# A decoder trunk in split float32: the first pass of each MLP takes two blocks by seven products, with a turned K tile and a split matmul in every fast pass

## The chip, the cores and the metric

The kernel runs on one core of one Trainium2 chip. The core has TensorE (matmuls, with a unit of its own for loading weights, PEld in the profile), VectorE (DVE), ScalarE (ACT), GpSimd (POOL), SyncE (SP), which issues the loads, and 16 DMA engines. Matmuls write into eight banks of PSUM, each 128 partitions by 512 float32 values. The metric is the time of one execution on the device, in microseconds (us).

## The reference

The input is 256 tokens of 2048 values. One layer mixes by a gated short convolution, one by multi-head latent attention; each is followed by an MLP with 8192 hidden values, and after each mixer and each MLP stands a layer norm of `ALPHA * x + f(x)`. The change touches the two MLPs alone:

```python
def sq_relu_mlp(x, w1, w2):
    return jnp.square(jax.nn.relu(x @ w1)) @ w2

for layer in range(DEPTH):
    ...
    h = layer_norm(ALPHA * h + mix, ln_g[layer, 0], ln_b[layer, 0])
    h = layer_norm(ALPHA * h + sq_relu_mlp(h, mlp_w1[layer], mlp_w2[layer]),
                   ln_g[layer, 1], ln_b[layer, 1])
```

## The kernel before, in words

**Split float32.** Every operand is held as two parts, `hi` (rounded by a copy on ScalarE, line 121) and `lo` (the rest, by a subtraction on VectorE, line 122); `split` makes both. A product is then three matmuls, hi by hi, hi by lo and lo by hi, added in the same bank. `dot` (line 281) issues these three, each of 512 columns. In the hidden products the two parts of the activations lie side by side, so `high` takes 512 columns at once and `low` the first 256; `mm_run` issues high and low in turn for 16 tiles of K.

**Weights.** They come through one `stream`, a list of pieces of 128 by 1024 values made at the start in the order of use. `take` hands out the next one and prepares those up to `LOOK = 5` ahead: a load into one of five `raw` slots by SP and a split into one of eight pairs of slots. An entry with two sources (`w2f`, `w2g`) is a pair for the seven products: `prepare` (line 135) makes of its two pieces four further factors, with one difference of 1024 columns (line 154), two of 512 (lines 157 and 160), three splits of 1024 and one of 512, whose target `t4` has a single slot.

**Passes.** An MLP is cut into `NQ = 8` passes over 1024 hidden values each (`QC = 8` tiles of 128). In each pass the hidden values are made first, by 8 units of two weight pieces, and the second products then add to the 256 by 2048 outputs in `acc`. These are four blocks of 512 columns (`NB`) by two halves of tokens. In the first pass (q = 0) the hidden products are `mm_wide` (`ps_g`, `ps_w`), from input that is not normalised yet; `weighted` corrects them, and the normalised input `xhl` for the other passes is made meanwhile by `ln.normal`, one tile of K at a time. The second products of the first and the last pass are `down`: per block 4 pieces, 8 tiles of K, two halves of tokens, 3 matmuls each, 48 in all. The first pass copies its sums into `acc` by ScalarE (line 573) and calls `normal()` twice behind each copy.

**The fast passes** (`FAST`, q = 1 to 6) do the second products of blocks 0 and 1 wholly by `fast_products`: for each pair of K tiles seven products (`FACTORS`) instead of eight, into seven banks, 4 x 7 x 3 = 84 matmuls (`ps_f`). Their left factors are the hidden values and four sums of them, `forms`, which `hidden` makes for each two tiles: four operations on 128 columns and a split of 512. Blocks 2 and 3 follow by `MIXED = "ppsp"`, one quarter by seven products, three by `down`'s way, in the four banks "22", "3", "2", "4"; the quarter adds the four `OWN` products "1", "5", "7", "6" in banks of their own. `keep` adds the banks to `acc` or, for `OWN`, to `sums` (line 588), which `fold` adds into `acc` in the last pass. In the second MLP `extra` puts eight transposes and two operations for the residual into the passes q = 1 to 4.

**Order.** Each engine works off its instructions in order. The tile framework orders them when the kernel is built, so that an engine's order is not wholly that of the source. In `products` each unit takes bank 0 or 1 by turns. In the first unit of q = 1, tile `TURNED = 2` issues low before high, so that two lows and then two highs stand next to each other; in the passes after it high and low alternate throughout.

The lines that the prediction's steps touch: 122 (lo of a split), 154, 157 and 160 (a pair's differences), 199 and 203 (high and low), 283 to 285 (`dot`), 338 (sum of a hidden product), 397 (`ln.prepare`), 466 to 471 (`normal`), 478 and 479 (`weighted`), 573 (copy into `acc`), 588 (`keep`), 662 to 666 (`forms`).

Of the kernel before, what the change touches and what calls it, by code (L numbers as in the profile page):

```python
# [16 lines left out]
P = 128  # L17
W = 256 + 2
T = 256
# [18 lines left out]
MIXED = "ppsp"  # L38
FIRST = (0, 1, 2, 4, 6, 8, 12, 16)
# [12 lines left out]
def trunk(ctx: ExitStack, tc: tile.TileContext, xT, vecs, w_first, w_in, w_out, w_kv, w_q, w_uk, w_uv,  # L52
# [242 lines left out]
    def down(x, put, n):  # L295

        ps = [psum("ps_d") for _ in range(2)]
# [21 lines left out]
    OWN, KEPT = ("1", "5", "7", "6"), (2, 3, 4, 5, 6, 7, 0)  # L319

# [232 lines left out]
    def mlp(idx, ln, blocks, fast, begin=None, extra=None):  # L553
# [27 lines left out]
        def keep(p, g, ps):  # L581
# [3 lines left out]
            if q == 1 and p in OWN:  # L585
# [4 lines left out]
        def down_pairs(h, forms):  # L590

            n = QC // 2
            ps = {p: psum(f"ps_f{p}", bank) for (p, _, _), bank in zip(FACTORS, KEPT)}
            for j in range(n):
                fast_products(ps, h, forms, j, ps if j == 0 else (), ps if j == n - 1 else ())
            for p in ps:
                keep(p, 0, ps[p])
            ps = {p: psum("ps_d", bank) for p, bank in zip(("22", "3", "2", "4"), (1, *KEPT))}
# [19 lines left out]
            for p in ("3", "2", "4", "22"):  # L618
                keep(p, 1, ps[p])
# [11 lines left out]
        for q in range(NQ):  # L631
            ht = act.tile([P, QC, 2 * T], F32R, tag="c", name=f"h{idx}_{q}")
            h = [ht[:, k, :] for k in range(QC)]
            forms = None
# [4 lines left out]
            def pair_tile(m):  # L639

                if m % 2 == 0:
                    pool = (act, "ab") if m % 4 else (fast, "fp")
                    t = pool[0].tile([P, 2 * T], F32, tag=pool[1], name="fp")
                    pair.append(t.rearrange("p (i t) -> p i t", i=2))
                return pair[-1]

            def hidden(m, ps, evac, *func):
                both = pair_tile(m) if forms is not None else None
                f = both[:, m % 2, :] if forms is not None else tmp.tile([P, T], F32, tag="fh", name="fh", bufs=3)
# [4 lines left out]
                if forms is None:  # L654
                    put_split(h[m], f)
                elif m % 2:
                    at = ht[:, m - 1:m + 1, :]
                    split(at[:, :, :T], at[:, :, T:], both)
                    (a11, a21), (a12, a22) = ((both[:, i, :P], both[:, i, P:]) for i in range(2))
# [455 lines left out]
```

## Time and profile before

| what | value |
|---|---|
| three runs | 2034.58, 2035.73 and 2036.16 us |
| their median | 2035.73 us |
| the profiled execution | 2035.76 us, its span 2034.0 us |
| instructions in the profile | 30032 |
| granted TensorE clock | 1.0 throughout |
| read from HBM | 381.25 MB, 188 GB/s over the span |

The page gives each engine's busy time as a share of the span, the granted clock of TensorE in 40 slices, and the chain of work that ended last, followed back from the end. A window's row gives its length, then each engine's busy time with the number of instructions, the granted clock, the share of the DMA engines and GB/s. A row of the timeline gives the start, the length, engine, source line, operation, output and inputs, shape and count, and in brackets the idle time before it and what ended that. Operations of one engine overlap at their ends, so a row of two or more gives the step from one to the next better than the length of one. Matmuls overlap likewise: one of 512 columns is shown with 0.39 us, but the next starts 0.23 us after it.

### The profile page before, as it was taken

How to read it: one execution, taken by the hardware profiler on the slowest of the kernel's cores; microseconds unless marked ns; L12 is line 12 of the kernel's file. 1: busy time of each engine (PE TensorE's matmuls, PEld its weight loads, DVE VectorE, ACT ScalarE, POOL GpSimd, SP SyncE). 2: the span in 40 equal slices, each digit the busy share in tenths (PEclk: the TensorE clock that was granted, in tenths of full speed). 3: DMA queues.
4: the chain of work that ended last, by engine and by line, in shares of the span. 5: the costliest groups of instructions: out<-in, count | busy, mean ns of one | idle time of the engine just before them, and what ended most of it. 6: DMA issues, size and time to landing. Idle time of an engine off the chain costs nothing.

```text
span 2034.0 us, 30032 instructions
## 1 busy us (share of the span) xinstructions
PE 2025.4 (100%) x11204; PEld 1756.3 (86%) x11204; DVE 1686.9 (83%) x2571; ACT 1198.7 (59%) x1829; POOL 2.3 (0%) x21
## 2 busy tenths in 40 slices
PE   9999999999999999999999999999999999999998
PEld 8888888988888888888889998898888888888886
DVE  7667677788898988989888988776889898898986
ACT  6444445676666565655656655566666656566561
POOL 0000000000000000000000000000000000000000
PEclk9999999999999999999999999999999999999999
DMA  8666666564746557465754534656474655746573
GB/s 309 200 188 187 188 193 189 177 196 127 265 147 216 187 177 250 150 222 165 254 171 160 180 118 145 187 179 194 131 244 145 227 193 161 255 150 214 181 237 121
DMA packets 106850, 385.31 MB, mean 189 GB/s; under 512 B 11856, under 2 KB 12752, under 8 KB 106448
## 3 DMA queue, kind: packets, MB, share of 16 engines
q1 hardware_dynamic: 106560, 383.27, 58.6%
q8 instruction: 88, 1.44, 0.3%
q14 instruction: 58, 0.48, 0.1%
q10 hardware_dynamic: 144, 0.13, 0.0%
HBM read 381.25 MB, written 2.10 MB: 188 GB/s over the span
## 4 chain that ended last, share of the span: by engine, by line
PE 93%; DVE 4%; DMA 1%; issue 1%; ACT 1%; DVEq 0%; ACTq 0%
PE ps_u L199 20%; PE ps_l L199 13%; PE ps_u L203 10%; PE ps_l L203 7%; PE ps_d L283 6%; PE ps_d L285 6%; PE ps_d L284 6%; PE ps_f L283 3%; PE ps_f L285 3%; PE ps_f L284 3%; PE ps_w L233 2%; PE ps_w L231 2%; PE ps_w L232 2%; DMA raw<-in_w_dram 1%; DVE lo L122 1%; PE ps_g L233 1%
## 5 line engine op out<-in xcount | busy, mean ns | idle before, releaser
L122 DVE TENSOR_TENSOR lo<-raw,hi 128x1024 fp32r<-128x1024 f32 x710 | 857.4, 1220 | 225.1 <-ACT hi L121 153.8
L121 ACT CAST hi<-raw 128x1024 fp32r<-128x1024 f32 x710 | 741.6, 1050 | 396.8 <-DMA raw<-in_w_dram 117.1
L199 PE MATMUL ps_u<-xhl,hi 128*128 128x512 f32 x1792 | 629.6, 396 | 1.9 <-DVE sums L588 1.9
L203 PE MATMUL ps_u<-xhl,lo 128*128 128x256 f32 x1792 | 502.0, 280 | 0.0
L199 PEld LDWEIGHTS ps_u<-xhl,hi 128*128 128x128 f32 x1792 | 336.1, 188 | 83.7 <-ACT hi L121 3.0
L203 PEld LDWEIGHTS ps_u<-xhl,lo 128*128 128x128 f32 x1792 | 338.4, 189 | 0.6
L199 PE MATMUL ps_l<-xhl_a,hi 128*128 128x512 f32 x704 | 244.1, 393 | 0.0
L283 PE MATMUL ps_d<-hi,h 128*128 128x512 f32 x556 | 217.5, 391 | 0.2 <-DVE sums L588 0.2
L285 PE MATMUL ps_d<-hi,h 128*128 128x512 f32 x556 | 216.6, 390 | 0.0
L284 PE MATMUL ps_d<-lo,h 128*128 128x512 f32 x556 | 216.6, 390 | 0.0
L203 PE MATMUL ps_l<-xhl_a,lo 128*128 128x256 f32 x704 | 195.4, 279 | 0.0
L199 PEld LDWEIGHTS ps_l<-xhl_a,hi 128*128 128x128 f32 x704 | 132.1, 188 | 29.8
L203 PEld LDWEIGHTS ps_l<-xhl_a,lo 128*128 128x128 f32 x704 | 131.9, 188 | 0.2
L121 ACT CAST hi_t<-raw_t 128x1024 fp32r<-128x1024 f32 x60 | 63.0, 1050 | 108.8 <-DVE raw_t L154 93.3
L283 PEld LDWEIGHTS ps_d<-hi,h 128*128 128x128 f32 x556 | 104.4, 188 | 22.6 <-DVE sums L588 0.7
L285 PEld LDWEIGHTS ps_d<-hi,h 128*128 128x128 f32 x556 | 104.4, 188 | 22.1
L284 PEld LDWEIGHTS ps_d<-lo,h 128*128 128x128 f32 x556 | 104.4, 188 | 21.7
L652 ACT ACTIVATE fp<-fp 128x256 f32<-128x256 f32 x96 | 40.0, 417 | 81.5 <-DVE fp L338 80.7
L199 PE MATMUL ps_l<-z,hi 128*128 128x512 f32 x240 | 82.4, 391 | 0.0
L154 DVE TENSOR_TENSOR raw_t<-raw,raw 128x1024 f32<-128x1024 f32 x60 | 73.1, 1219 | 7.4 <-DMA raw<-in_w2f_dram 7.3
L122 DVE TENSOR_TENSOR lo_t<-raw_t,hi_t 128x1024 fp32r<-128x1024 f32 x60 | 73.2, 1220 | 1.3
L233 PE MATMUL ps_w<-xd,hi 128*128 128x258 f32 x256 | 72.9, 285 | 0.0
(270 smaller groups left out, 3359.9 us busy)
## 6 DMA issues: line engine op xcount, KB each, us to landing
raw<-in_w_dram SPq DMA_DIRECT2D x392, 512.0 KB, 4.5
raw<-in_w2f_dram SPq DMA_DIRECT2D x96, 512.0 KB, 3.7
raw<-in_w_in_dram SPq DMA_DIRECT2D x88, 512.0 KB, 4.3
raw<-in_w_out_dram SPq DMA_DIRECT2D x32, 512.0 KB, 4.2
raw<-in_w_o_dram SPq DMA_DIRECT2D x32, 512.0 KB, 4.0
raw<-in_w2g_dram SPq DMA_DIRECT2D x24, 512.0 KB, 5.0
raw<-in_w_kv_dram SPq DMA_DIRECT2D x10, 512.0 KB, 3.6
raw<-in_w_q_dram SPq DMA_DIRECT2D x8, 512.0 KB, 4.2
```

Source lines behind the costliest of these rows:

```text
L121: nc.scalar.copy(hi, src)
L122: nc.vector.tensor_tensor(lo, src, hi.bitcast(F32), ALU.subtract)
L154: nc.vector.tensor_tensor(t.rearrange(two, a=2), b12.unsqueeze(1).to_broadcast([P, 2, BW]), r1.rearrange(two, a=2), ALU.subtract)
L199: nc.tensor.matmul(ps, w[blk // 8][0][:, blk % 8, :], x, start=first, stop=False)
L203: nc.tensor.matmul(ps[:, :T], w[blk // 8][1][:, blk % 8, :], x[:, :T], start=False, stop=last)
L231: nc.tensor.matmul(ps[:, :W], hi, x[k][:, :W], start=k == 0, stop=False)
L232: nc.tensor.matmul(ps[:, :W], lo, x[k][:, :W], start=False, stop=False)
L233: nc.tensor.matmul(ps[:, :W], hi, x[k][:, W:], start=False, stop=k == NC - 1)
L283: nc.tensor.matmul(ps, x[0], w[0], start=first, stop=False)
L284: nc.tensor.matmul(ps, x[0], w[1], start=False, stop=False)
L285: nc.tensor.matmul(ps, x[1], w[0], start=False, stop=last)
L652: nc.scalar.activation(f, f, AF.Relu)
```

## The change

Four things are done together. The first pass of each MLP takes blocks 2 and 3 by `down` as before, but blocks 0 and 1 by the seven products; its hidden values are held in pairs, in a part of `sums` that is free by then, and its `forms` are made behind the last hidden product. The sums of these seven products are copied by ScalarE, and the one part of `acc` that they don't reach is set to zero by GpSimd; three calls of `normal()` instead of two stand behind each copy of a block. Second, the tile `TURNED` is used in all passes from q = 1 on. Third, one matmul of each fast pass (tile 7 of product "22") is cut into two of 256 columns (`EVEN`). Fourth, the `OWN` products of the fast passes take the banks 0, 5, 6, 7 instead of 5, 6, 7, 0, and `keep` is called for each two of "22", "3", "2", "4" right behind their last product. In the pass q = 1 the sums of the first four `OWN` products are now added by VectorE, no longer copied by ScalarE.

```diff
+EVEN = (QC - 1, "22")
...
-            if q not in FAST:
+            if q == NQ - 1:
                 out += halves(w2[l, q])
                 continue
+            if q == 0:
+                out += halves(w2[l, q, 2:])
             out += [(w2f[l, q, j, 0], w2f[l, q, j, 1]) for j in range(QC // 2)]
-            for j, kind in enumerate(MIXED):
+            for j, kind in enumerate(MIXED if q else ""):
...
-    def dot(ps, w, x, first, last):
+    def dot(ps, w, x, first, last, two=False):
         nc.tensor.matmul(ps, x[0], w[0], start=first, stop=False)
-        nc.tensor.matmul(ps, x[0], w[1], start=False, stop=False)
+        for at in (slice(0, T), slice(T, 2 * T)) if two else (slice(None),):
+            nc.tensor.matmul(ps[:, at], x[0], w[1][:, at], start=False, stop=False)
         nc.tensor.matmul(ps, x[1], w[0], start=False, stop=last)
...
+    OWN_BANKS = (0, 5, 6, 7)
...
                 nc.scalar.copy(block(n, t), ps)
-                for _ in range(2):
+                for _ in range(3):
                     normal()
...
-            if q == 1 and p in OWN:
+            if q == 0 or q == g == 1 and p in OWN:
                 nc.scalar.copy(at, ps)
...
-        def down_pairs(h, forms):
+        def first_pair(h, forms, banks):
             n = QC // 2
-            ps = {p: psum(f"ps_f{p}", bank) for (p, _, _), bank in zip(FACTORS, KEPT)}
+            ps = {p: psum(f"ps_f{p}", bank) for (p, _, _), bank in zip(FACTORS, banks)}
             for j in range(n):
                 fast_products(ps, h, forms, j, ps if j == 0 else (), ps if j == n - 1 else ())
             for p in ps:
                 keep(p, 0, ps[p])
+
+        def second_pair(h, forms):
...
-                        ps.update({p: psum(f"ps_f{p}", bank) for p, bank in zip(OWN, KEPT[3:])})
+                        ps.update({p: psum(f"ps_f{p}", bank) for p, bank in zip(OWN, OWN_BANKS)})
...
-                            dot(ps[p], wide_rows(w, kk), held(h[k], t), k == 0, k == QC - 1)
+                            dot(ps[p], wide_rows(w, kk), held(h[k], t), k == 0, k == QC - 1, (k, p) == EVEN)
+                    if j == n - 1:
+                        for _, p in two:
+                            keep(p, 1, ps[p])
...
-            for p in ("3", "2", "4", "22"):
-                keep(p, 1, ps[p])
...
+            firsts, forms = sums[:, 0:2].rearrange("p i g c -> p (i g) c"), None
...
+                    if q == 0:
+                        t = firsts[:, m // 2]
...
+            def form(j):
+                (a11, a21), (a12, a22) = ((pair[j][:, i, :P], pair[j][:, i, P:]) for i in range(2))
+                sf = fast.tile([P, 4, P], F32, tag="sf", name="sf")
...
+                split(forms[:, j, 0, :], forms[:, j, 1, :], sf.rearrange("p i c -> p (i c)"))
...
                 acc = act.tile([P, 2, D], F32, tag="a1", name=f"acc{idx}")
+                forms = act.tile([P, QC // 2, 2, 4 * P], F32R, tag="a2", name=f"forms{idx}_{q}")
+                nc.gpsimd.memset(block(1, 1), 0.0)
+                for j in range(QC // 2):
+                    form(j)
...
-                for m, ps in enumerate(products(QC, xhl, TURNED if q == 1 else None, (0, 1))):
+                for m, ps in enumerate(products(QC, xhl, TURNED, (0, 1))):
...
-            if q in FAST:
-                down_pairs(h, forms)
+            if q == 0:
+                down(h, put, 2, (2, 3))
+                down(h, put, 3, (1, 7))
+                first_pair(h, forms, (0, 2, 3, 4, 5, 6, 7))
             else:
-                for n in range(NB):
-                    down(h, put, n)
+                first_pair(h, forms, KEPT)
+                second_pair(h, forms)
```

More of the change, by code (lines that the diff above doesn't have):

```diff
@@ L293, in wide_rows, with down @@
         return [v[:, 4 * kk:4 * kk + 4, :].rearrange("p a c -> p (a c)") for v in w]
-    def down(x, put, n):
-        ps = [psum("ps_d") for _ in range(2)]
+    def down(x, put, n, banks=(None, None)):
+        ps = [psum("ps_d", bank) for bank in banks]
         for j in range(len(x) // 2):
@@ L597, in down_pairs @@
                 keep(p, 0, ps[p])
+        def second_pair(h, forms):
+            n = QC // 2
             ps = {p: psum("ps_d", bank) for p, bank in zip(("22", "3", "2", "4"), (1, *KEPT))}
@@ L633, in mlp @@
             h = [ht[:, k, :] for k in range(QC)]
-            forms = None
+            firsts, forms = sums[:, 0:2].rearrange("p i g c -> p (i g) c"), None
             if q in FAST:
@@ L653, in hidden @@
                 nc.scalar.activation(f, f, AF.Square)
-                if forms is None:
+                if both is None:
                     put_split(h[m], f)
@@ L658, in hidden @@
                     split(at[:, :, :T], at[:, :, T:], both)
-                    (a11, a21), (a12, a22) = ((both[:, i, :P], both[:, i, P:]) for i in range(2))
-                    sf = fast.tile([P, 4, P], F32, tag="sf", name="sf")
-                    s1, s2, s3, s4 = (sf[:, i, :] for i in range(4))
-                    nc.vector.tensor_tensor(s1, a21, a22, ALU.add)
-                    nc.vector.tensor_tensor(s3, a21, a11, ALU.subtract)
-                    nc.vector.tensor_tensor(s2, s1, a11, ALU.subtract)
-                    nc.vector.tensor_tensor(s4, a12, s2, ALU.subtract)
-                    split(forms[:, m // 2, 0, :], forms[:, m // 2, 1, :], sf.rearrange("p i c -> p (i c)"))
+                    if q:
+                        form(m // 2)
             if q == 0:
```

14 lines of the change are left out of this document (10 added, 4 removed).

## The prediction

> **What bounds the kernel now.** I read the page's engine shares first, then the chain of waits, then busy time in windows cut at the stage borders, then the timelines of TensorE and VectorE at those borders.
>
> ```profile
> PE 2025.4 (100%) x11204; PEld 1756.3 (86%) x11204; DVE 1686.9 (83%) x2571; ACT 1198.7 (59%) x1829; POOL 2.3 (0%) x21
> PEclk9999999999999999999999999999999999999999
> PE 93%; DVE 4%; DMA 1%; issue 1%; ACT 1%; DVEq 0%; ACTq 0%
> ```
>
> TensorE is busy all the time at the full granted clock, and 93% of the chain is its own. So a change gains what it takes out of TensorE's stream, and loses where TensorE is made to wait. VectorE, at 83%, is the candidate for such waits. The sum is made against the profiled execution, 2035.76 us (span 2034.0 and 1.76 around it); the median of the three runs, 2035.73, is the same. About 0.2%, or 4.1 us, is what a measurement of this kernel can tell from no change: below 2031.7 is faster, above 2039.8 slower.
>
> **The hidden products (K tile turned in every pass).** These are windows over the 256 matmuls of `ps_u` in the passes q = 1 to 7 of both MLPs (window, length, PE, PEld, DVE, ACT):
>
> ```profile
> 454.80:499.19 44.39, 44.39 (x256) 39.01 (x255) 2.91 (x7) 2.51 (x7) 1.00 0.46 134
> 539.94:585.15 45.21, 45.21 (x256) 39.12 (x255) 2.92 (x7) 2.54 (x7) 1.00 0.54 171
> ...
> 969.74:1014.95 45.21, 45.21 (x256) 39.12 (x255) 2.92 (x7) 2.55 (x7) 1.00 0.77 246
> 1414.86:1459.25 44.39, 44.39 (x256) 39.01 (x255) 2.92 (x7) 2.51 (x7) 1.00 0.46 134
> 1500.89:1546.10 45.21, 45.21 (x256) 39.08 (x255) 2.92 (x7) 2.56 (x7) 1.00 0.52 160
> 1587.92:1632.37 44.45, 44.45 (x256) 39.08 (x256) 2.93 (x7) 2.53 (x7) 1.00 0.55 177
> ...
> 1761.94:1807.24 45.30, 45.30 (x256) 39.16 (x256) 2.92 (x7) 2.55 (x7) 1.00 0.54 178
> 1849.11:1893.57 44.46, 44.46 (x256) 38.74 (x256) 2.91 (x7) 2.52 (x7) 1.00 0.56 181
> 1934.31:1979.52 45.21, 45.21 (x256) 39.12 (x255) 2.93 (x7) 2.55 (x7) 1.00 0.74 234
> ```
>
> The same 256 matmuls take 44.39 us in both passes with the turned tile (q = 1) and 45.21 or 45.30 in nine of the twelve without; the other three, 44.45, follow a wait of TensorE. The entries of a turned and an unturned pass:
>
> ```profile
> 455.03 0.28 PE L203 MATMUL ps_u<-xhl,lo 128*128 128x256 f32 x1
> 455.14 0.40 PE L199 MATMUL ps_u<-xhl,hi 128*128 128x512 f32 x1
> 455.37 0.40 PE L203 MATMUL ps_u<-xhl,lo 128*128 128x256 f32 x2
> 540.17 0.28 PE L203 MATMUL ps_u<-xhl,lo 128*128 128x256 f32 x1
> 540.28 0.40 PE L199 MATMUL ps_u<-xhl,hi 128*128 128x512 f32 x1
> 540.51 0.28 PE L203 MATMUL ps_u<-xhl,lo 128*128 128x256 f32 x1
> ```
>
> Up to the third tile both run in the same steps (0.11 us, then 0.23), so an unturned pass is in the state in which the turn has worked two times out of two. The changed order has the turn in all fourteen passes. The split matmul makes a fast pass 434 matmuls instead of 433, so every entry falls on the same parity of the count as the two that worked; that is the only use I can see for it. Gain: the first MLP's six at 45.21 save 6 x 0.82 = 4.9; the second's save 0.82 + 0.91 + 0.82 = 2.6, and 0.06 or 0.07 each at the three after a wait, 0.2. Together 7.6 us; the bounds are 0 and 7.6.
>
> [...]
>
> The split adds one matmul in each of twelve passes. Two of 256 columns step by about 0.115 us each (540.17 to 540.28), one of 512 by 0.23 (540.28 to 540.51): nothing to 0.03 us each, so 0.2 us for all; no more than 12 x 0.05 = 0.6.
>
> **The banks and the order of `keep`.** Second halves of the fast passes, the first from the first MLP, the rest q = 1 to 5 of the second, and the entry of the pass behind q = 4:
>
> ```profile
> 604.64:625.90 21.26, 21.26 (x94) 17.47 (x93) 20.30 (x24) 11.08 (x12) 0.00 (x0) 1.00 0.69 238
> 1478.74:1500.89 22.15, 22.15 (x102) 18.30 (x101) 20.31 (x22) 15.81 (x20) 0.00 (x0) 1.00 0.79 271
> 1565.59:1587.92 22.33, 22.33 (x103) 18.15 (x101) 20.57 (x26) 11.54 (x12) 0.00 (x0) 1.00 0.65 225
> 1651.86:1674.40 22.54, 22.36 (x103) 18.08 (x101) 21.58 (x27) 11.56 (x12) 0.00 (x0) 1.00 0.68 229
> 1738.34:1761.94 23.60, 22.64 (x102) 18.06 (x101) 21.94 (x27) 12.22 (x13) 0.00 (x0) 1.00 0.67 227
> 1826.72:1849.11 22.39, 21.43 (x95) 17.32 (x93) 19.82 (x24) 10.56 (x12) 0.00 (x0) 1.00 0.63 219
> 1761.94 0.47 PE L199 MATMUL ps_u<-xhl,hi 128*128 128x512 f32 x1 [0.72 <-DVE sums L588]
> 1759.92 1.87 DVE L588 TENSOR_TENSOR sums<-sums,ps_f 128x512 f32<-128x512 f32 x3
> ```
>
> Against the undisturbed 22.15 (with the residual's transposes) and 21.26 (without), the last four are longer by 0.18 + 0.39 + 1.45 + 1.13 = 3.15 us. TensorE waits for bank 0, which holds product "6", the last of four that VectorE adds up: the three at 1759.92 end at 1761.79. In the change bank 0 holds "1", the first added, three adds (1.8 us) earlier; the largest of these waits, the 1.45 of q = 4, is shorter than that. One part of the 3.15, some 0.5 us in q = 4, lies at the start of its half and isn't of bank 0. I take 2.6 of 3.15; the bounds are 0 and 3.15. In q = 1 four copies move from ScalarE to VectorE adds (2.4 us); the passes from q = 2 on carry these already, the first MLP's at 21.26 without a wait, so they cost nothing; were they uncovered, 2.4 per MLP.
>
> **The first pass by seven products.** Its second products before, the 84 matmuls of a fast half, and the stretch in which VectorE works without a pause:
>
> ```profile
> 411.05:454.80 43.75, 43.75 (x194) 36.20 (x193) 35.95 (x67) 31.98 (x50) 0.00 (x0) 1.00 0.63 199
> 1371.31:1414.86 43.55, 43.55 (x194) 36.04 (x193) 31.09 (x51) 31.84 (x49) 0.00 (x0) 1.00 0.66 197
> 499.19:518.68 19.49, 19.49 (x87) 15.80 (x85) 18.06 (x24) 13.00 (x19) 0.00 (x0) 1.00 0.57 190
> 388.24:439.81 51.57, 51.57 (x318) 46.60 (x317) 51.19 (x107) 46.06 (x87) 0.00 (x0) 1.00 0.60 189
> ```
>
> On TensorE, 192 matmuls become 96 + 84: 43.75 / 2 + 19.49 = 41.4 against 43.75 and 43.55, a gain of 2.4 and 2.2. But VectorE is saturated just there, and the change gives it more. Two blocks' weights, eight splits, become four pairs, each with four operations of 1024 columns (three splits and a difference) and three of 512; the forms come on top, four of 128 and a split of 512 for each of four. What one operation takes in a full queue:
>
> ```profile
> 388.24 0.75 DVE L478 TENSOR_TENSOR t<-ps_g,ab 128x256 f32<-128x256 f32 x2 [0.95 <-ACT ab L452]
> 388.91 0.87 DVE L479 SCALAR_TENSOR_TENSOR t<-ab,wgb,t 128x256 f32<-128x256 f32 x2
> 439.81 1.23 DVE L122 TENSOR_TENSOR lo<-raw,hi 128x1024 fp32r<-128x1024 f32 x1
> 511.72 2.35 DVE L122 TENSOR_TENSOR lo<-raw,hi 128x1024 fp32r<-128x1024 f32 x2
> 507.85 0.28 DVE L665 TENSOR_TENSOR sf<-fp,sf 128x128 f32<-128x128 f32 x1
> 508.05 0.68 DVE L157 TENSOR_TENSOR raw<-raw,raw_t 128x512 f32<-128x512 f32 x1
> 1348.13 0.76 DVE L478 TENSOR_TENSOR t<-ps_g,ab 128x256 f32<-128x256 f32 x2 [0.20 <-ACT ab L452]
> ```
>
> One behind the other: 1024 columns 1.136, 512 columns 0.60 (the three adds above: (1.87 - 0.68)/2), 256 columns 0.336, the three-operand ones of L479 0.40, 128 columns 0.20. Built, the changed kernel's VectorE has, from the first `t` of the pass (388.24, which nothing before it changes) to the last factor of the last pair, 25 of 1024, 20 of 512, 63 of 256, 8 of L479's kind and 16 of 128: 28.4 + 12.0 + 21.2 + 3.2 + 3.2 = 68.0 us, to 456.3. The same sum for before, over its 19, 81 and 8 to the split at 439.81, gives 440.2, and that split ends 0.7 later, so I add 0.7: 457.0. TensorE alone would be there at 411.05 + 41.4 = 452.4. So it waits, and the pass ends with VectorE. The next pass needs one more split (1.14) before its first low product, at 458.2, which stood at 455.03: **3.1 us later**, not 2.4 earlier. In the second MLP seven operations of 256, the next norm's differences, are missing: 65.7 from 1348.13 is 1413.8, with the 0.7 and the split 1415.7, against 1414.86 + 0.23 = 1415.1: 0.6 later. Together +3.7. The bounds: -4.6, if the queue runs ahead of my sum, and what the buffers can do (below). ScalarE's additions (by my count, pairs and forms +8.0, seven copies for four +1.5) bring its 31.98 us to some 41.5 of 46: behind VectorE, so nothing; TensorE would pay for what it is late. Block 2 takes a bank from which the last hidden unit is read only at about 412.9 (first MLP); the wait of 1.2 us lies in the 4.6 that TensorE waits for VectorE anyway, so it costs nothing, 1.2 without that cover. Normalising three tiles behind each block instead of two adds none. The zeroing on GpSimd (2.3 us busy in all) is read a pass later. On SP's queue 16 loads change source, none is added.
>
> **Sum.** 2035.76 - 7.6 + 0.2 - 2.6 + 3.7 = 2029.5 us.
>
> **Rivals.**
> 1. The turn carries over to no further pass: which of the two lengths a pass settles in is decided by more than order and count. For it: three unturned passes have the short length and one, 45.30, behind the same kind of wait has not. Against: both turned ones have it. Time: 2029.5 + 7.6 = 2037.1, no change. [...]
> 2. VectorE isn't late: the forms and pairs fit into its pauses. For: its window at 499.19 to 518.68 takes pairs with 18.06 of 19.49 busy and no wait. Against: the queue sum, which holds for before to 0.7 us. Time: 2035.76 - 7.6 + 0.2 - 2.6 - 4.6 = 2021.2.
> 3. The other side: buffers pace the pairs. A pair needs three of five raw slots and three of eight split slots, and a single slot for its last factor, freed by TensorE, which is itself late; each pair then waits for the one before. In the fast pass of before, differences of two pairs start at
>
> ```profile
> 487.32 1.22 DVE L154 TENSOR_TENSOR raw_t<-raw,raw 128x1024 f32<-128x1024 f32 x1
> 494.71 1.21 DVE L154 TENSOR_TENSOR raw_t<-raw,raw 128x1024 f32<-128x1024 f32 x1
> 506.71 1.22 DVE L154 TENSOR_TENSOR raw_t<-raw,raw 128x1024 f32<-128x1024 f32 x1
> ```
>
> 7.4 and then 12.0 us apart; my sum has 6.3. At 9 us each of three gaps in each MLP costs 2.7: 2029.5 + 16.2 = 2045.7. It makes the kernel slower from 8.0 us a gap on ((2039.8 - 2029.5) / 6 = 1.7 more). Against: by the queue's times each slot is free before VectorE gets to it.
>
> **How the numbers follow.** Forecast 0.52, rival 1 0.20, rival 2 0.14, rival 3 0.14. The forecast's own spread, a partial turn (four of nine passes) or 1 us of VectorE's queue in either MLP, is 2026 to 2033; I put 0.42 of its 0.52 below 2031.7. Faster: 0.42 + 0.14 = 0.56. Same: 0.10 + 0.20 and a little of rival 3, 0.31. Slower: 0.13. The range, 2022.5 to 2038.5, holds rival 1 and half of rival 2 and leaves out the other half and rival 3.
>
> **What would show it.** Right: all `ps_u` windows at 44.4; no wait on `sums` ahead of `ps_u`; in the first pass `ps_f` with waits for `lo_t`, `lo` and `t`, some 5 us in the first MLP and 2 to 3 in the second, VectorE without a pause from the first `t` to the last factor. Wrong: passes still at 45.2 (rival 1), a first pass of 41.4 (rival 2), pauses of VectorE between the pairs, with TensorE or ScalarE named as what ended them (rival 3).

## The result and the profile after

The changed kernel takes 2042.72 us (median of 6 runs, 2041.05 to 2045.59) against 2036.51 for the kernel before on the same chips (6 runs, 2034.58 to 2039.69): a ratio of 1.0033, 95% interval 1.0023 to 1.0042. It is slower by some 6.7 us, where the sum on record has 6.3 us of gain. The profiled execution took 2041.05 us, its span is 2039.3.

Engine shares and the chain of waits on the page of the changed kernel:

```profile
PE 2021.6 (99%) x11192; PEld 1751.1 (86%) x11192; DVE 1730.6 (85%) x2651; ACT 1212.0 (59%) x1843; POOL 3.3 (0%) x23
PE 75%; DVE 15%; DMA 4%; issue 3%; ACT 3%; SPq 0%; DVEq 0%; ACTq 0%
```

TensorE is busy 3.8 us less than before, yet the span is longer. Its share of the chain fell from 93% to 75% and VectorE's rose from 4% to 15%: the chain now leaves TensorE and comes back to it. Where it does so is in the list of TensorE's waits (engine, line, what it waited for: us in total, times, longest):

```profile
PE ps_f L286 <- ACT hi_t L124: 4.8, 4, 1.6
PE ps_d L286 <- DVE sums L593: 4.6, 6, 1.2
```

The waits of `ps_u` for `sums`, which the prediction set out to remove, are gone. The first line is the first pass by seven products. In the second the products of blocks 2 and 3, `ps_d`, wait for adds of `keep`, in six of the twelve fast passes. The kernel before has one such wait, in q = 4 of the second MLP:

```profile
PE ps_d L283 <- DVE sums L588: 0.2, 1, 0.2
```

(Line numbers are 3 to 5 higher than before; L593 is the add of `keep`, L125 the lo of a split, L286 the first matmul of `dot`.)

The stages, as windows of the changed kernel (columns as before: window, length, PE, PEld, DVE, ACT, POOL, clock, DMA): the two first passes, the two stretches from the first hidden product of q = 1 to the last of q = 7, then the hidden products of q = 3 in the first MLP and of q = 4 in the second.

```profile
411.44:457.92 46.48, 43.55 (x184) 33.25 (x182) 46.48 (x86) 34.61 (x54) 0.00 (x0) 1.00 0.35 102
1374.30:1419.77 45.47, 42.69 (x183) 33.33 (x181) 44.91 (x80) 33.78 (x54) 0.00 (x0) 1.00 0.32 104
457.92:1017.97 560.05, 557.28 (x2861) 473.48 (x2861) 508.38 (x674) 351.24 (x501) 0.53 (x1) 1.00 0.62 204
1419.77:1984.89 565.12, 562.97 (x2893) 477.02 (x2892) 510.03 (x673) 351.51 (x501) 0.00 (x0) 1.00 0.61 201
628.41:672.80 44.39, 44.39 (x257) 39.14 (x256) 38.95 (x56) 28.72 (x47) 0.00 (x0) 1.00 0.56 182
1680.12:1725.62 45.50, 45.44 (x258) 39.11 (x256) 39.99 (x57) 28.13 (x47) 0.00 (x0) 1.00 0.55 181
```

And the same two stretches of the kernel before, with its hidden products of q = 3:

```profile
454.80:1014.95 560.15, 560.15 (x2855) 473.99 (x2854) 497.57 (x654) 348.20 (x498) 0.53 (x1) 1.00 0.60 196
1414.86:1979.52 564.66, 562.56 (x2887) 476.27 (x2886) 502.19 (x662) 348.09 (x498) 0.00 (x0) 1.00 0.60 194
625.90:671.11 45.21, 45.21 (x257) 39.20 (x256) 40.15 (x59) 28.98 (x46) 0.00 (x0) 1.00 0.57 179
```

Against before, the first passes cost 46.48 - 43.75 = 2.7 and 45.47 - 43.55 = 1.9 us. The stretches behind them are 0.1 shorter and 0.5 longer, though the hidden products in the first MLP do take 44.4 us. The opening is 0.4 later. Together 5.4 of the 5.3 us between the two profiled executions. So there are two questions: why nothing is left of the turn's 0.82 us a pass, and why the first pass is dearer than the 3.7 of the prediction.

The first question has its answer at the middle of those six passes. Timeline of TensorE and VectorE of the changed kernel, third fast pass of the first MLP (start, length, engine, line, operation, in brackets the idle time before and its releaser):

```profile
694.80 0.39 PE L289 MATMUL ps_d<-hi,h 128*128 128x512 f32 x1
695.75 0.50 PE L286 MATMUL ps_d<-hi,h 128*128 128x512 f32 x1 [0.56 <-DVE sums L593]
...
690.35 0.69 DVE L125 TENSOR_TENSOR t<-raw,t 128x512 fp32r<-128x512 f32 x1 [1.05 <-ACT t L124]
690.96 2.41 DVE L125 TENSOR_TENSOR lo<-raw,hi 128x1024 fp32r<-128x1024 f32 x2
693.88 1.22 DVE L125 TENSOR_TENSOR lo<-raw,hi 128x1024 fp32r<-128x1024 f32 x1 [0.51 <-ACT hi L124]
695.02 1.88 DVE L593 TENSOR_TENSOR sums<-sums,ps_f 128x512 f32<-128x512 f32 x3
```

The third group of `ps_d` ("2") takes bank 3, which holds product "1" of the first half. VectorE adds that up only behind four operations of preparing weights. The same place in the timeline of the kernel before, where the first half began at 671.11 instead of 672.80, the ends of the two rows of q = 3 above:

```profile
686.61 0.69 DVE L588 TENSOR_TENSOR acc<-acc,ps_f 128x512 f32<-128x512 f32 x1 [1.24 <-PE ps_f L285]
687.21 0.68 DVE L122 TENSOR_TENSOR t<-raw,t 128x512 fp32r<-128x512 f32 x1
687.82 2.35 DVE L122 TENSOR_TENSOR lo<-raw,hi 128x1024 fp32r<-128x1024 f32 x2
690.55 1.22 DVE L122 TENSOR_TENSOR lo<-raw,hi 128x1024 fp32r<-128x1024 f32 x1 [0.38 <-ACT hi L121]
691.69 1.87 DVE L588 TENSOR_TENSOR sums<-sums,ps_f 128x512 f32<-128x512 f32 x3
...
693.34 0.39 PE L283 MATMUL ps_d<-hi,h 128*128 128x512 f32 x1
```

The order on VectorE is the same in both kernels: the add of "3", then t, three lo's (0.60 + 3 x 1.136 = 4.0 us), then the add of "1". Before, that add was done at about 692.3 (691.69 plus one step of 0.6) and TensorE asked for the bank at 693.34, 1.0 us later. After, the add starts 22.22 us into the half instead of 20.58, ends at about 695.7, and TensorE, which would have asked at 695.03, starts at 695.75. The margin was 1.0 us; VectorE came 1.64 later relative to TensorE. The turn takes 0.82 us in every pass from the time that VectorE has to get there, and 1.64 is what the passes q = 2 and 3 take together. The pass falls back to 86 us. By the same reckoning the margin before is 0.9 to 1.5 us in the first MLP's passes q = 2 to 6; in the second MLP it is 0.25 in q = 3 and used up in q = 4, which is the one wait there.

### The profile page after: what moved, and what is told of

Its sections match the earlier page's. It is cut to its first block, busy times and chain, and to the rows that moved or that the text cites. A ratio compares the mean times of both kernels' runs of the same rounds, so it can differ in the third digit from the quotient of the medians.

```text
span 2039.3 us, 30076 instructions
## 1 busy us (share of the span) xinstructions
PE 2021.6 (99%) x11192; PEld 1751.1 (86%) x11192; DVE 1730.6 (85%) x2651; ACT 1212.0 (59%) x1843; POOL 3.3 (0%) x23
## 4 chain that ended last, share of the span: by engine, by line
PE 75%; DVE 15%; DMA 4%; issue 3%; ACT 3%; SPq 0%; DVEq 0%; ACTq 0%
PE ps_u L202 15%; PE ps_l L202 13%; PE ps_u L206 8%; PE ps_l L206 7%; DVE lo L125 5%; PE ps_d L286 4%; PE ps_d L288 4%; PE ps_d L289 4%; DMA raw<-in_w_dram 3%; PE ps_f L289 2%; PE ps_f L288 2%; PE ps_f L286 2%; ACT hi L124 2%; DVE lo_t L125 2%; DVE raw_t L157 1%
## 5 line engine op out<-in xcount | busy, mean ns | idle before, releaser
L125 DVE TENSOR_TENSOR lo<-raw,hi 128x1024 fp32r<-128x1024 f32 x710 | 858.0, 1221 | 186.0 <-ACT hi L124 114.9
L286 PE MATMUL ps_d<-hi,h 128*128 128x512 f32 x492 | 193.7, 394 | 4.6 <-DVE sums L593 4.6
L288 PE MATMUL ps_d<-lo,h 128*128 128x512 f32 (+1 forms) x504 | 192.3, 385 | 0.0
L289 PE MATMUL ps_d<-hi,h 128*128 128x512 f32 x492 | 191.9, 390 | 0.0
L124 ACT CAST hi_t<-raw_t 128x1024 fp32r<-128x1024 f32 x68 | 71.3, 1049 | 114.4 <-DVE raw_t L157 108.6
L286 PEld LDWEIGHTS ps_d<-hi,h 128*128 128x128 f32 x492 | 92.4, 188 | 26.9 <-DVE sums L593 7.7
L288 PEld LDWEIGHTS ps_d<-lo,h 128*128 128x128 f32 x504 | 94.7, 188 | 19.6
L289 PEld LDWEIGHTS ps_d<-hi,h 128*128 128x128 f32 x492 | 92.4, 188 | 19.2
L157 DVE TENSOR_TENSOR raw_t<-raw,raw 128x1024 f32<-128x1024 f32 x68 | 83.0, 1220 | 8.6 <-DMA raw<-in_w2f_dram 8.6
L125 DVE TENSOR_TENSOR lo_t<-raw_t,hi_t 128x1024 fp32r<-128x1024 f32 x68 | 82.9, 1220 | 1.4 <-ACT hi_t L124 0.4
```

The lines of the kernel that those rows point to most:

```text
L124: nc.scalar.copy(hi, src)
L125: nc.vector.tensor_tensor(lo, src, hi.bitcast(F32), ALU.subtract)
L157: nc.vector.tensor_tensor(t.rearrange(two, a=2), b12.unsqueeze(1).to_broadcast([P, 2, BW]), r1.rearrange(two, a=2), ALU.subtract)
L288: nc.tensor.matmul(ps[:, at], x[0], w[1][:, at], start=False, stop=False)
```

## The experiments

Theory A: VectorE is full over a whole pass, so whatever TensorE saves comes back as a wait. Theory B: the banks and the new order of the adds make the waits. Theory C: only the order of VectorE's queue at the middle of the pass does, which the kernel before has too. All ratios are to the kernel before on the same chip, with 95% intervals.

**1. The turn alone.** The kernel before, and

```diff
-products(QC, xhl, TURNED if q == 1 else None, (0, 1))
+products(QC, xhl, TURNED, (0, 1))
```

> The kernel before, with the turned tile in all passes from q = 1 and nothing else of the change. Theory A (the fast passes are paced by VectorE and not by TensorE's matmuls, so what the turn saves in a pass comes back as a wait for VectorE): the hidden products show 44.4 us a pass, yet the time is within 1.5 us of before. Theory B (the turn saves its 7.6 us, and the banks and the order of the adds that came with it lose them): 7.6 us faster than before, 2029. Theory C (the place of four operations ahead of the second add on VectorE makes the wait, which the kernel before has too): between, 2 to 5 us faster.

Measured: 2032.59 us (11 runs, 2030.26 to 2036.84), ratio 0.9983 (0.9974 to 0.9992): 3.5 us faster. Half of the turn's 7.6 is there, half isn't. A's band and B's time are both missed; C's band holds it. The trace of experiment 1 is of its fastest execution (2030.26 us). There TensorE is busy 5.7 us less (2019.7 against 2025.4), with a turned pass of the first MLP still at 45.21 us (625.26 to 670.47), and the late adds hold `ps_d` up by some 0.6 us in all. So how the median loses half is not seen in it.

**2. The first pass alone.** The changed kernel, and

```diff
-products(QC, xhl, TURNED, (0, 1))
+products(QC, xhl, TURNED if q == 1 else None, (0, 1))
-OWN_BANKS = (0, 5, 6, 7)
+OWN_BANKS = (5, 6, 7, 0)
-dot(..., (k, p) == EVEN)
+dot(...)
```

with the adds of "3", "2", "4", "22" behind the loop again.

> The changed kernel with the turn in q = 1 only, no split matmul, the old banks and the old order of the adds: the first pass by seven products alone. All theories: 4.6 us slower than before (2.7 in the first MLP, 1.9 in the second), about 2041. If the first pass had cost the 3.7 of the prediction: 2040. If it costs nothing by itself and only disturbs what comes behind it: within 1 us of before.

Measured: 2043.18 us (8 runs), ratio 1.0031 (1.0021 to 1.0041): 6.3 us slower, more than the 4.6 expected. Its first passes are those of the changed kernel:

```profile
411.17:457.63 46.46, 43.54 (x183) 33.23 (x181) 46.46 (x86) 34.60 (x54) 0.00 (x0) 1.00 0.35 101
1374.16:1419.61 45.45, 42.67 (x183) 33.29 (x181) 44.90 (x80) 33.79 (x54) 0.00 (x0) 1.00 0.34 103
```

**3. Everything but the first pass.** The changed kernel with q = 0 by `down` for all four blocks, as before.

> The changed kernel with the first pass as before: turn, split matmul, banks and order of the adds. Theory A: within 1.5 us of before, with waits of the second block's products for the adds of 4 to 8 us in sum. Theory B: the same time, but then the turn alone is 7 us faster. The prediction's sum without its term for the first pass: 10.0 us faster, 2026.

Measured: 2036.02 us (11 runs), ratio 0.9994 (0.9986 to 1.0003). Turn, banks, order and split together are worth nothing that can be told from no change: what the turn alone gains is mostly lost again by the other three (0.9994 - 0.9983, 2.2 us, though the two intervals overlap). The time lies in A's band, with waits for the adds of 3.9 us in sum, just under the 4 to 8 that A named; this run alone doesn't refute A. Behind the longest of these waits, 1.8 us, nine matmuls take 3.75 us instead of 9 x 0.23 = 2.1 (last section).

**4. Priority for the adds.** The changed kernel; the same work, another order on VectorE. (In the first pass the edit covers ScalarE's copies of `keep` too.)

```diff
+            with tc.high_priority():
                 for p in ps:
                     keep(p, 0, ps[p])
```

> The changed kernel with the seven adds behind the first half given priority, so that one operation instead of four stands between the first and the second of them on VectorE; same work in all. Theory A (VectorE is full over the whole pass): the waits of the second block's products for these adds go, waits for lo parts or in the hidden products come instead, and the time is within 1.5 us of the changed kernel. Theory C (only the order is at fault): the waits, 7.3 us in sum (0.3 to 1.6 each), go and nothing comes instead: 7 us faster than the changed kernel, some 2 faster than before.

Measured: 2037.94 us (11 runs), ratio 1.0003 (0.9994 to 1.0012), where the changed kernel has 1.0033: 6 us faster than that. C expected 7. The first MLP's stretch:

```profile
459.42:1014.79 555.37, 555.37 (x2860) 473.47 (x2859) 507.54 (x674) 351.63 (x499) 0.53 (x1) 1.00 0.63 205
```

555.4 instead of 560.1 us: six passes at 85.2, with the same VectorE time (507.5 against 508.4). There A is refuted: the operations fit, only their order didn't. In the second MLP the stretch is only 1.2 us shorter than the changed kernel's 565.12, and `ps_d` now waits for lo parts, as A expected:

```profile
1416.59:1980.51 563.92, 561.15 (x2893) 476.23 (x2892) 509.00 (x673) 351.35 (x500) 0.00 (x0) 1.00 0.62 202
PE ps_d L288 <- DVE lo L125: 2.7, 4, 0.9
```

So in the changed kernel's second MLP the order of these adds is not all.

**5. Turn and priority, nothing else.** The kernel before with the edits of 1 and 4.

> The kernel before with the turn in all passes and priority for the seven adds behind the first half; the first pass, the banks and the adds of the second half as before. If the order of VectorE's queue is what holds the turn's gain back (theory C): hidden products of 44.4 us in all passes, second halves without a wait, the second MLP's fast stretch some 2 to 3 us shorter than with the turn alone; 2029 to 2031 us. If the priority only shifts the waits to the lo parts that now stand behind the adds (theory A): 2032 to 2034, as with the turn alone.

Measured: 2027.79 us (5 runs, 2026.57 to 2029.12), ratio 0.9961 (0.9949 to 0.9974): 8.2 us faster than before, faster than either kernel and below the 2029 to 2031 that C expected. Against experiment 1 that is some 4.5 us, by intervals that touch at 0.9974. VectorE at the same place and the first matmul of block "2", in the timeline:

```profile
685.88 0.69 DVE L588 TENSOR_TENSOR acc<-acc,ps_f 128x512 f32<-128x512 f32 x1 [0.61 <-PE ps_f L285]
687.01 0.69 DVE L122 TENSOR_TENSOR t<-raw,t 128x512 fp32r<-128x512 f32 x1 [0.45 <-ACT t L121]
687.62 1.88 DVE L588 TENSOR_TENSOR sums<-sums,ps_f 128x512 f32<-128x512 f32 x3
...
692.61 0.39 PE L283 MATMUL ps_d<-hi,h 128*128 128x512 f32 x1
```

The list of TensorE's waits names three, all outside the fast passes: `offset` 1.4, `warm` 1.1 and `ps_g` 0.9 us. The two stretches as windows:

```profile
455.71:1011.24 555.53, 555.53 (x2855) 473.34 (x2854) 496.47 (x654) 347.63 (x498) 0.53 (x1) 1.00 0.60 198
1411.26:1971.39 560.13, 560.13 (x2887) 476.80 (x2886) 500.71 (x662) 347.75 (x498) 0.00 (x0) 1.00 0.59 196
```

The add of "1" now starts at 687.62, one operation behind that of "3" and 5.0 us ahead of the `ps_d` that needs its bank. No wait of `ps_d` or `ps_u` is left, and the two stretches are 4.6 and 4.5 us shorter than before. That is 9.1 of 7.6 + 2.6 = 10.2: the turn's gain and that of the bank waits, without the new banks.

**6. Work moved to GpSimd.** Experiment 4 with `normal`'s two operations in the MLPs on GpSimd.

```diff
-nc.vector.tensor_tensor(u, d, self.A, ALU.mult)
-nc.vector.tensor_tensor(u, u, self.B, ALU.add)
+nc.gpsimd.tensor_tensor(u, d, self.A, ALU.mult)
+nc.gpsimd.tensor_tensor(u, u, self.B, ALU.add)
```

> The changed kernel with priority for the adds, and the two VectorE operations of `normal` in the MLPs (256 columns each, up to 32 in an MLP) issued on GpSimd instead. If VectorE's queue paces the first pass (the prediction's step): the 46.5 and 45.5 us of its second products go to 42 to 43, some 6 us in both MLPs, 2031 to 2033 in all. If buffers or the place of the casts on ScalarE pace it: within 1 us of the kernel with the priority alone, 2038, with pauses on VectorE in the first pass. If GpSimd's operations are long or slow VectorE's down (0.41 us for 256 columns becomes more): no gain or a loss, with TensorE waiting for the normalised input at the first hidden product of q = 1.

Measured: 2051.62 us (5 runs), ratio 1.0073 (1.0061 to 1.0086): some 14 us slower than experiment 4. The third expectation held in the time but not in its wait: the longest waits of TensorE are those of `ps_d` for hidden values in the first passes (`t` 5.6 us, `h` 4.8 us), and none is for the normalised input. Nor does this tell queue from buffers; what its trace shows of VectorE and of the clock stands in the last section.

**7. Turn and banks.** Experiment 1 with the banks.

```diff
-zip(OWN, KEPT[3:])
+zip(OWN, OWN_BANKS)
```

> The kernel before with the turn in all passes and the banks 0, 5, 6, 7 for the OWN products; the adds at the end of the second half in their old order, no split matmul. The turn alone was 2032.6, with banks, order of the adds and split 2036.0. If the banks are what costs: 2035 to 2036, with waits of the second block's products for the adds. If the order of the adds (or the split) is what costs: 2032 to 2033, or less by the wait of 1.2 us in sum for bank 0 that the turn alone still has.

Measured: 2031.67 us (11 runs), ratio 0.9976 (0.9967 to 0.9985). The banks lose nothing; what they gain against experiment 1, 0.9976 to 0.9983, lies within the intervals. The trace does have waits for the adds, as the first expectation said, though not its time:

```profile
PE ps_d L283 <- DVE sums L589: 5.7, 7, 1.2
```

Experiment 1's trace has 1.2 us of waits of `ps_u` for bank 0 instead, and 0.1 of these. But that is the fastest of its eleven executions and this the slowest of eleven (2034.63 us), so whether the banks bring these waits stays open.

**8. VectorE relieved in the first pass.** Experiment 4 without `normal`'s two operations.

```diff
-nc.vector.tensor_tensor(u, d, self.A, ALU.mult)
-nc.vector.tensor_tensor(u, u, self.B, ALU.add)
```

> The changed kernel with priority for the adds, with the two VectorE operations of `normal` left out in both MLPs (`xhl` is made of the values that are not normalised): 32 operations of 0.336 us, 10.7 us of VectorE's first pass in each MLP, and nothing put in their place. If VectorE's queue paces the first pass: its second products go from 46.5 and 45.5 us to 41.4 to 42.5, the waits for hi_t and lo_t go, 2029 to 2031 in all. If the buffers, or the place of the casts behind the copies on ScalarE, pace it: still above 45, VectorE then with pauses, 2036 to 2038.

Measured: 2030.26 us (7 runs), ratio 0.9969 (0.9958 to 0.998): 7 us faster than experiment 4. Its first passes:

```profile
410.75:452.44 41.69, 41.69 (x182) 33.92 (x181) 40.37 (x66) 26.65 (x37) 0.00 (x0) 1.00 0.47 145
1367.81:1409.12 41.31, 41.31 (x182) 33.84 (x181) 35.96 (x50) 26.74 (x37) 0.00 (x0) 1.00 0.48 149
```

41.7 and 41.3 us, what TensorE alone needs by the prediction's 41.4, and no wait of `ps_f` is left. (Behind it the first MLP's q = 1 takes 88.6 us where experiment 4 has 85.0, so a part is lost again.) But more went out of the pass than the 32 operations. Without the norm's statistics to wait for, the rest of `normal` ran ahead of the pass as well and was done by 376 us in the first MLP: 16 more operations of VectorE and 32 of ScalarE, whose busy time in the first of these windows falls from 34.2 to 26.7 us. So this shows that the work of `normal` makes the pass late, but by itself it doesn't show through which of the two engines. The changed kernel's trace speaks for VectorE: in the first MLP it has no pause in this pass, while ScalarE stands idle and waits for a difference that VectorE makes:

```profile
444.99 1.04 ACT L124 CAST hi_t<-raw_t 128x1024 fp32r<-128x1024 f32 x1 [2.18 <-DVE raw_t L157]
```

**9 and 10. The order of the second half's adds, and the split, each on experiment 5.**

```diff
+                    if j == n - 1:
+                        for _, p in two:
+                            keep(p, 1, ps[p])
-            for p in ("3", "2", "4", "22"):
-                keep(p, 1, ps[p])
```

> The kernel with turn and priority (2027.8), with the adds of the second half's "22", "3", "2", "4" moved to where the change has them, behind each two products. Turn, banks, split and this order together lost 3.4 us to the turn alone, the banks none of it. If the order loses them: 2030 to 2032, in the second MLP's passes above all. If it is the split, or if the priority already cures this loss too: 2027 to 2029.

Measured: 2028.47 us (5 runs), ratio 0.9961 (0.9947 to 0.9975).

```diff
-dot(ps[p], wide_rows(w, kk), held(h[k], t), k == 0, k == QC - 1)
+dot(ps[p], wide_rows(w, kk), held(h[k], t), k == 0, k == QC - 1, (k, p) == EVEN)
```

> The kernel with turn and priority (2027.8) and the split matmul. By the prediction's step 0.2 us slower, no more than 0.6: 2027.5 to 2028.5, unless it settles the entry of a pass that has the long length (one of the twelve that the turn should reach still has 45.2): then 0.8 faster. If the split is what lost the 3.4 us: 2030 to 2032.

Measured: 2029.33 us (5 runs), ratio 0.9966 (0.9954 to 0.9979). With the priority in place neither can be told from none; experiment 9 fits its second band, and 10 lies between its two. Nor does the split settle the length of every pass: in experiment 10 one hidden product of the second MLP still takes 45.30 and one 45.25 us.

**11. The first pass on experiment 5.** Experiment 2 with the edits of 1 and 4.

> The kernel with turn and priority (2027.8) and the first pass by seven products; old banks, old order of the second half's adds, no split. If the first pass costs by itself what its windows showed, 2.7 and 1.9, and no more: 2032 to 2033. If it costs the 6.3 of the kernel with this part alone, with a part lost behind it: 2034. If with the priority nothing of it is left behind the pass but banks and order of the adds lose something in it: 2032 against the 2037.9 of the changed kernel with priority.

Measured: 2035.88 us (11 runs), ratio 0.9996 (0.9987 to 1.0004): 7 us slower than experiment 5, more than expected. Its trace has the second MLP's 45.5 us again and, behind the longest wait of the first pass, something new:

```profile
454.30:457.60 3.30, 3.24 (x8) 2.57 (x9) 3.30 (x4) 2.05 (x4) 0.00 (x0) 0.52 0.53 158
...
1416.96:1462.14 45.18, 45.18 (x258) 39.21 (x256) 40.65 (x56) 33.73 (x52) 0.00 (x0) 1.00 0.66 223
```

For 3.3 us the granted clock is 0.52, and 8 matmuls take the time of some 14 (last section). The second row is the first hidden product behind the second MLP's first pass: turned, and yet 45.18 us. Against experiment 5's trace q = 1 of the first MLP begins 3.6 us later, and the second MLP's stretch takes 562.9 us instead of 560.1. So the first pass costs more than its own windows.

**12. Turn, banks and order of the adds, without priority and split**: experiment 7 with the edit of 9.

> The kernel before with turn, banks 0, 5, 6, 7 and the adds of the second half behind each two products; no priority, no split. With turn and banks alone 2031.7, with the split besides these three 2036.0. If the order of the adds loses the difference: 2035 to 2037. If the split, which fixes the entry of every pass so that each comes half a microsecond to a microsecond sooner on a late VectorE: 2031 to 2033. If both have a part: 2033 to 2035.

Measured: 2034.00 us (11 runs), ratio 0.9987 (0.9978 to 0.9996): 0.0011 above experiment 7, which lacks the order, and 0.0007 below 3, which has the split besides. That fits the third expectation, that both have a part, but the interval overlaps those of 7 and of 3, so neither part is shown.

## Why the prediction was wrong

**The turn: effect right, its gain given back.** The tile shortens the hidden products as forecast: 11 of 14 take 44.3 to 44.6 us, and the rival that it carries over to no further pass is out. Three in the second MLP do not: 45.21, 45.50 and 45.49, the last two with 0.06 and 0.2 us of idle time inside. Which entry settles the long length stays open; a turned pass of 45.21 us without a wait in the pass ahead of it (85.14 of 85.14 us busy) occurs in experiment 1 too. Why the order of one tile settles the length of 256 matmuls no run shows. (The term's parts, 4.9, 2.6 and 0.2, add up to 7.7; the 0.1 changes nothing.) But -7.6 stood in the sum as a net gain. Alone it brought 3.5 us (experiment 1); with the order of VectorE's queue mended, it and the bank waits together brought 8 (experiment 5).

**The step that failed** is the one under "The banks and the order of `keep`", and with it the -7.6 taken as a net gain. It priced the second halves by their "undisturbed 22.15 (with the residual's transposes) and 21.26 (without)", looked at bank 0 ahead of `ps_u`, and asked of no other bank by how much it came in time; the sum has no term for a wait in the middle of a pass. The one such wait of before it saw and set aside: the "some 0.5 us in q = 4" that "lies at the start of its half and isn't of bank 0" is `ps_d` at bank 3. In the pass shown above bank 3 was in time by 1.0 us; with two turned passes TensorE asks for it 1.64 us sooner relative to VectorE, and waits. In the changed kernel these late adds are what cost: experiment 4 has the same work in another order and is some 6 us faster. For the turn alone the cause rests on times (experiment 5 against 1), since the trace of 1 has hardly any of these waits. What the trace of before showed, four operations of 4.0 us between the adds of "3" and "1" with a margin of 1 us behind them, was enough to doubt the -7.6.

**The banks.** The waits ahead of `ps_u` went, and for the reason given. The gain of 2.6 did not come: with the turn, the banks moved the time from 0.9983 to 0.9976, and order and split, the other two parts, back to 0.9994. In experiment 5's trace priority for the adds of the first half took the same waits away without them, so VectorE's order could do what the banks were to do (0.4 to 0.7 us of these waits is left in the traces of 9, 10 and 11).

**The split** was sized at 0.2, at most 0.6. Its ratio is 0.0005 above experiment 5's and 0.0007 above 12's, 1.0 and 1.4 us; the intervals allow 0.2, so this stays open.

**The copies of q = 1** cost nothing, as forecast: in experiment 2, where the pass has them and not the turn, its second products take 40.75 us in the first MLP, as before.

**The first pass.** In the first MLP the term held: VectorE works without a pause from the first `t` to the last factor (0.03 us of pauses in sum), and 3.1 measured 2.7, or 3.1 with the opening's 0.4. TensorE's waits stand under another name than forecast, `hi_t` and `hi` of ScalarE instead of `lo_t`, `lo` and `t`, with 2.9 us in the first MLP and 2.8 in the second where 5 and 2 to 3 were named. The second MLP's 0.6 measured 1.9. There VectorE did pause, 1.2 us in sum, 0.64 of it for `xhl` and 0.39 for `hi_t`, both made by ScalarE, which had copied two sums of `ps_f` just ahead of that `hi_t`:

```profile
1415.68 1.23 DVE L125 TENSOR_TENSOR lo_t<-raw_t,hi_t 128x1024 fp32r<-128x1024 f32 x1 [0.39 <-ACT hi_t L124]
```

So in the second MLP what was mis-sized is a term at nothing, ScalarE's additions "behind VectorE, so nothing". In all +3.7 measured +6.3 (experiment 2): 4.6 in the two first passes and, in that kernel's trace, 1.4 in the second MLP's stretch behind:

```profile
1419.61:1985.65 566.04, 565.32 (x2887) 477.19 (x2886) 510.38 (x673) 353.55 (x501) 0.00 (x0) 1.00 0.62 201
1419.61:1464.82 45.21, 45.21 (x258) 39.22 (x257) 41.04 (x58) 33.80 (x53) 0.00 (x0) 1.00 0.67 224
```

566.04 against 564.66, with the first MLP's unchanged (560.16). The seven hidden products of the second MLP, 45.21 to 45.30 us each, all have the long length here: q = 1, turned but entered behind a product of seven, 45.21 instead of 44.39, and q = 3, 45.30 instead of the 44.45 of before. So VectorE sets the end of the first MLP's pass as forecast, the second MLP's size was too small by 1.3 us, and what the pass does to the lengths behind it had no term.

**The rivals.** Buffers didn't pace the pairs: VectorE had no pause in the first MLP's first pass (46.48 of 46.48 us busy). That VectorE would not be late is out too. None of the three was what happened: a wait of `ps_d` for a late add in the middle of six of the twelve fast passes.

**The chain of kernels.** Each with one part more, by the ratios: turn -3.5 us, banks -1.4, order of the second half's adds +2.2, split +1.4, first pass +7.9; the changed kernel is at +6.7. Against the sum on record, -7.6, -2.6 for banks and order, +0.2 and +3.7, the first two lines miss by 4 and 3.4 us, the last by 4.2, of which about half is seen in the windows of the first passes and the lengths behind them. Each step carries two intervals of some 1.8 us to either side: the turn and the first pass are clear of that, banks, order and split each are not.

## What to carry to other kernels

When TensorE's stream gets shorter, check for each buffer that it reuses by how much the engine that frees it came in time, not only whether there was a wait; here a margin of 1.0 us did not carry two passes' gain of 0.82 each. Where a wait appears though the freeing engine has idle time, look at the order of its queue first: an add that frees a bank belongs ahead of the preparing of later weights, and here that one edit took 6 us off the changed kernel. Before a shorter algorithm goes onto TensorE, look whether the engine that makes its operands has room in that very stage; here VectorE had next to none (busy 46.48 of 46.48 us in the first MLP, 44.91 of 45.47 in the second), and the two first passes took 4.6 us longer.

## What the runs showed of the hardware

While GpSimd worked, some of VectorE's operations took longer. In experiment 6 an operation of 256 columns takes GpSimd 0.98 us; VectorE takes 0.41 for the same one in experiment 4 (line, engine, operation, count, busy us and mean ns of one):

```profile
L472 POOL TENSOR_TENSOR nu<-nu,ab 128x256 f32<-128x256 f32 x32 | 31.4, 984 | 2.2
```

VectorE's own groups meanwhile, in the window from 388 to 432 us of experiment 6:

```profile
L476 DVE TENSOR_TENSOR xhl<-xres,xhl 128x256 fp32r<-128x256 f32 x12 | 9.2, 780 | 0.0
L125 DVE TENSOR_TENSOR h<-sums,h 128x512 fp32r<-128x512 f32 x4 | 4.4, 1088 | 0.0
L483 DVE TENSOR_TENSOR t<-ps_g,ab 128x256 f32<-128x256 f32 x3 | 1.2, 415 | 1.0 <-ACT ab L457 1.0
```

and in the same window of experiment 4, where VectorE does `nu` itself:

```profile
L472 DVE TENSOR_TENSOR nu<-nu,ab 128x256 f32<-128x256 f32 x14 | 5.7, 413 | 0.0
L476 DVE TENSOR_TENSOR xhl<-xres,xhl 128x256 fp32r<-128x256 f32 x13 | 5.3, 414 | 0.1
L125 DVE TENSOR_TENSOR h<-sums,h 128x512 fp32r<-128x512 f32 x4 | 2.7, 684 | 0.0
```

`xhl` and `h`, both of whose inputs lie in SBUF, go from 0.41 to 0.78 and from 0.68 to 1.09 us; `t`, with an input in PSUM (`ps_g`), keeps its 0.41 (0.42 in experiment 4). GpSimd's last `nu` of that pass in experiment 6 ends at 431.61 us; the `xhl` that starts at 432.09 takes 0.41 again, and `forms` of 512 columns 0.68 at 434.70, where the one at 430.94 took 1.23. Why these are slowed and `t` is not was not shown. The first passes of experiment 6 take 51.1 and 52.0 us, where experiment 4 has 46.7 and 45.4. The granted clock in them is 0.90 and 0.93, against 0.96 and 1.00 there, and its mean over an execution 0.995 or 0.996, against 0.998 to 1.0, so a part of the 14 us may be clock.

Behind a wait of 1.6 to 1.8 us TensorE's granted clock was about half for some 3.3 us in three traces, those of experiments 3, 4 and 11, and full in that of the changed kernel. Experiment 4 and the changed kernel have the same wait of 1.62 us in the first pass; first the windows of experiment 4:

```profile
452.00:455.40 3.40, 1.69 (x6) 0.99 (x7) 3.40 (x6) 3.40 (x5) 0.00 (x0) 1.00 0.61 170
455.40:458.70 3.30, 3.30 (x10) 2.61 (x9) 2.50 (x4) 2.72 (x5) 0.00 (x0) 0.52 0.73 211
```

and of the changed kernel:

```profile
452.00:455.40 3.40, 1.62 (x6) 0.92 (x7) 3.40 (x6) 3.40 (x5) 0.00 (x0) 1.00 0.59 171
455.40:458.70 3.30, 3.30 (x17) 2.59 (x16) 3.30 (x4) 3.20 (x6) 0.00 (x0) 1.00 0.69 204
```

After nearly the same idle time one gets through 10 matmuls in 3.3 us, the other through 17: 7 x 0.23 = 1.6 us. In experiment 3 a wait of `ps_d` has the same sequel in the middle of a pass; the granted clock is 0.61 in the window from 1740.50 to 1744.10, which begins 0.5 us ahead of the first matmul behind the wait, and the step goes from 0.23 to 0.43 us:

```profile
1740.50:1744.10 3.60, 3.11 (x8) 2.47 (x9) 3.60 (x7) 0.00 (x0) 0.00 (x0) 0.61 0.57 206
1738.56 0.39 PE L286 MATMUL ps_d<-lo,h 128*128 128x512 f32 x1
1738.78 0.39 PE L287 MATMUL ps_d<-hi,h 128*128 128x512 f32 x1
1740.99 0.56 PE L284 MATMUL ps_d<-hi,h 128*128 128x512 f32 x1 [1.82 <-DVE sums L591]
1741.35 0.63 PE L286 MATMUL ps_d<-lo,h 128*128 128x512 f32 x1
1741.78 0.63 PE L287 MATMUL ps_d<-hi,h 128*128 128x512 f32 x1
...
1744.34 0.57 PE L287 MATMUL ps_d<-hi,h 128*128 128x512 f32 x1
1744.74 0.40 PE L284 MATMUL ps_d<-hi,h 128*128 128x512 f32 x1
```

So the length of the wait alone doesn't decide: the same 1.62 us stands ahead of 0.52 in experiment 4 and of 1.00 in the changed kernel. What decides was not shown.

In experiment 2 the four executions with a mean granted clock of 1.0 take 2039.8 to 2043.0 us, the four with 0.999 take 2043.4 to 2045.8, and the profiled one, whose windows were read above, is of the first kind. In experiment 11 time and clock don't go together like this: 2036.79 us has 1.0, 2033.14 has 0.999. So how much of the first pass's price is clock stays open. The clock is not what spreads experiment 1 over 6.6 us: all eleven executions there have 1.0. That spread stays open.
